# Taps of a 31-wide convolution on three engines, with sums in PSUM, and more first products in three passes

## The chip, the cores and the metric

The kernel runs on one core of a Trainium2 chip. The metric is device time in microseconds (us) for one execution, taken over several executions; the median is compared. A profiled execution of the same program gives the trace from which the rows below come. The engines are TensorE (PE, with its weight loads as PEld), VectorE (DVE), ScalarE (ACT), GpSimd (POOL) and SyncE (SP), which issues the loads.

## The reference

One inference step of a two-layer trunk on 256 prompt tokens and 8 sample tokens, 264 columns in all, of width 2048. Layer 0 mixes tokens with a Conformer convolution, layer 1 with a gated linear recurrence; each is followed by a convolutional feed-forward block of width 5632. The change touches the first mixer alone:

```python
def conformer_conv(x, buf, w_pw1, b_pw1, w_dw, b_dw, ln_g, ln_b, w_pw2, b_pw2):
    h = x @ w_pw1 + b_pw1                    # 2048 -> 4096
    a, gt = jnp.split(h, 2, axis=-1)
    u = a * jax.nn.sigmoid(gt)
    c, new_buf = causal_depthwise_conv(u, buf, w_dw, b_dw)   # 31 taps a channel
    c = jax.nn.silu(layernorm(c, ln_g, ln_b))
    return c @ w_pw2 + b_pw2, new_buf
```

The prompt starts with an empty history, so tap d of a prompt column reads the column d places earlier and nothing where that lies ahead of the prompt. Each sample token has its own history of 30 columns (buf), which enters as one weighted sum a channel.

## The kernel before, in words

Channels lie on the 128 partitions, so the 2048 channels are 16 tiles (KT) of 128 x 264 (T). Everything stays in SBUF between stages; weights stream in as 128 x 2048 blocks of 1 MB into three buffers (tag w), the loads issued by SyncE in one fixed order up to four slots ahead (LOADS).

A **slot** (L185) is one product of such a block with 16 slices. A weight in NATIVE is multiplied as fp32, 16 matmuls, each two records in the trace. Any other is split: ScalarE rounds it to a high part (split_hi, L139), VectorE subtracts to get the low part (split_lo, L151), and three passes of 16 matmuls run (high x high, high x low, low x high; L181 to L183), for which the right-hand side has to be in two parts too. In the stage of the change, all 32 first products (pw1) are native and all but two of the second products (pw2) are split.

For channel tile i there are two slots: the product a (index i) and the product for the gate (index 16 + i). After the matmuls of a slot the program issues what was registered with `later(n, ...)` (0 is the next slot, 1 the one after it): first the list "begin", then the casts of weights two slots ahead (AHEAD), then "early", then the low parts, then "late" (L198 to L206). The order on ScalarE, VectorE and TensorE is that order of issue, since the schedule is manual for them.

For tile i this is: sigmoid of the gate product (ScalarE, L366), the gate u = (a + b) x sigmoid (VectorE, L374), then the taps. One sum starts as ScalarE's scaling of u (L378), the other (part) on VectorE; 29 further taps (L409, L417) are VectorE's multiply-and-add, alternating between the two sums, in three groups over the next three slots; an addition joins the sums (L425, and its twin for the last tile, L421). The last tile, of which nothing can be put beside a product, has 17 of its taps (TE) on TensorE with diagonal weights, made by ScalarE beforehand (diagonals, L388; diagonal_taps, L395).

From tile 5 on, a mean m0 of the first four tiles is subtracted within the sums; the first five tiles have it subtracted in one block (catch_up, L449). Squares (ScalarE, L348) and two running sums (dsum and qsum, VectorE, L358 and L359) feed the LayerNorm, whose totals come from TensorE after the last tile (p_mu, L499). At the start, conv_state multiplies the sample history with the weights (L339) and reduces it over 30 places (L341), and normalise (L457 on) makes the 16 normalised right-hand sides xg, once the RMSNorm's scale is known; tile 0 is multiplied before that, by the unscaled xr.

PSUM has eight banks: six in one rotation (tag pt, L73), one for statistics (st), one (pl) for a transposed piece of the output at the very end. GpSimd does nothing in this stage.

Of the kernel before, what the change touches and what calls it, by code (L numbers as in the profile page):

```python
# [17 lines left out]
P = 128  # L18
# [5 lines left out]
CW = 31  # L24
# [20 lines left out]
NATIVE = {("pw1", n) for n in range(2 * KT)} | {("pw2", 0), ("pw2", 1), ("ho", 0)}  # L45
AHEAD = 2
LOADS = 4
TE = 17
# [14 lines left out]
def kernel(ctx: ExitStack, tc: tile.TileContext, a: dict):  # L63
    nc = tc.nc
    vec, act, pe = nc.vector, nc.scalar, nc.tensor
    ctx.enter_context(tc.manual_schedule(engines={mybir.EngineType.PE, mybir.EngineType.Activation, mybir.EngineType.DVE}))
# [20 lines left out]
    def pcol(name, i):  # L87
        c = COL[name] + i
        return par[:, c : c + 1]
# [134 lines left out]
    class Stats:  # L224
# [91 lines left out]
    with ExitStack() as ph:  # L316
        gp = ph.enter_context(tc.tile_pool(name="gp", bufs=1))
        cstate = gp.tile([P, KT, CW - 1, NB], F32, tag="cstate", name="cstate")
# [19 lines left out]
        def conv_state():  # L338
            vec.tensor_tensor(out=cstate, in0=cstate, in1=wall[:, :, : CW - 1].unsqueeze(3).to_broadcast((P, KT, CW - 1, NB)),  # L339
                              op=ALU.mult)  # L340
            vec.tensor_reduce(out=csum, in_=cstate.rearrange("p k j b -> p k b j"), axis=AX.X, op=ALU.add)  # L341

        NM = 4
        c, m = [], {}

# [22 lines left out]
        def glu(i, pa):  # L368
            sg = m.pop(("sg", i))
            u = gp.tile([P, T], F32, tag="u", name=f"u{i}", bufs=3)  # L370
# [3 lines left out]
            vec.scalar_tensor_tensor(out=u, in0=pa[:, :T], scalar=pcol("b_pw1", i), in1=sg, op0=ALU.add, op1=ALU.mult)  # L374
            m[i] = u
            ci = gp.tile([P, T], F32, tag=f"c{i}", name=f"c{i}")
            c.append(ci)
            act.activation(ci, u, AF.Identity, scale=pcol("w_dw", i * CW + CW - 1), bias=pcol("b_dw", i))  # L378
            act.copy(ulast[:, i, :], u[:, SEQ - CW + 1 :])
# [4 lines left out]
        def diagonals():  # L384
            free = [sp.tile([P, 2, P], F32, tag=f"l{k}", name=f"diag{k}") for k in range((TE + 1) // 2)]
            for j in range(TE):
                diag[j] = free[j // 2][:, j % 2, :]
                act.activation(diag[j], ident, AF.Identity, scale=pcol("w_dw", (KT - 1) * CW + j))  # L388

        def diagonal_taps():  # L390
            u = m[KT - 1]
            pt = m["pt"] = bank("p_taps")
            for j in range(TE - 1, -1, -1):
                d = CW - 1 - j
                pe.matmul(pt[:, d:SEQ], diag[j], u[:, : SEQ - d], start=(j == TE - 1), stop=(j == 0))  # L395

        def taps(i, lo, hi):

            u, ci = m[i], c[i]
            if hi == CW - 1:  # L400
                part = m["part", i] = gp.tile([P, T], F32, tag="part", name=f"part{i}", bufs=2)
                w = pcol("w_dw", i * CW + CW - 2)
                if i <= NM:
                    vec.memset(part[:, :1], 0.0)
                    vec.tensor_scalar(out=part[:, 1:SEQ], in0=u[:, : SEQ - 1], scalar1=w, scalar2=None, op0=ALU.mult)
                    vec.tensor_copy(part[:, SEQ:], csum[:, i, :])
                else:
                    m0 = m["m0"]
                    vec.scalar_tensor_tensor(out=part[:, 1:SEQ], in0=u[:, : SEQ - 1], scalar=w, in1=m0[:, 1:SEQ],  # L409
                                             op0=ALU.mult, op1=ALU.subtract)  # L410
                    vec.tensor_scalar(out=part[:, :1], in0=m0[:, :1], scalar1=-1.0, scalar2=None, op0=ALU.mult)
                    vec.tensor_tensor(out=part[:, SEQ:], in0=csum[:, i, :], in1=m0[:, SEQ:], op=ALU.subtract)
                hi -= 1
            for j in range(hi - 1, lo - 1, -1):
                d = CW - 1 - j
                dst = ci if d % 2 == 0 else m["part", i]
                vec.scalar_tensor_tensor(out=dst[:, d:SEQ], in0=u[:, : SEQ - d], scalar=pcol("w_dw", i * CW + j),  # L417
                                         in1=dst[:, d:SEQ], op0=ALU.mult, op1=ALU.add)
            if lo == TE and i == KT - 1:
                d = CW - TE  # L420
                vec.tensor_tensor(out=ci, in0=ci, in1=m.pop(("part", i)), op=ALU.add)  # L421
                vec.tensor_tensor(out=ci[:, d:SEQ], in0=ci[:, d:SEQ], in1=m["pt"][:, d:SEQ], op=ALU.add)
                square(i)
            elif lo == 0:
                vec.tensor_tensor(out=ci, in0=ci, in1=m.pop(("part", i)), op=ALU.add)  # L425
                if i > NM:
                    square(i)
# [35 lines left out]

        later(0, normalise, last=True)
        later(2, conv_state, last=True)
        for i in range(KT):
            first = i == 0
            if i == 1:
                nc.sync.dma_start(cst, a["cst"])
                nc.sync.dma_start(a["o_conv_old"], a["cs"][:, :, 1:, :])  # L470
            pa, = slot([("pw1", i)], None, xr if first else xg)
            pg, = slot([("pw1", KT + i)], None, xr if first else xg, ahead=AHEAD if i < KT - 1 else 0)
            later(0, lambda i=i, pg=pg: sigmoid(i, pg), first=True)
            later(0, lambda i=i, pa=pa: glu(i, pa))
            if i == KT - 1:
                later(0, diagonal_taps)
                later(0, lambda i=i: taps(i, TE, 30), last=True)
                continue
            later(0, lambda i=i: taps(i, 16, 30), last=True)
            later(1, lambda i=i: taps(i, 3, 16))  # L480
            later(2, lambda i=i: taps(i, 0, 3))
            later(2, lambda i=i: gathered(i), last=True)
# [8 lines left out]
        mu = gp.tile([P, T], F32, tag="mu", name="mu")  # L491
# [39 lines left out]
        hl = nxt  # L531

# [460 lines left out]
    with ExitStack() as ph:  # L993
# [11 lines left out]
        pl = ps.tile([P, 512], F32, tag="pl", name="p_y", bufs=1)  # L1005
# [10 lines left out]
        for i in range(2):  # L1016
            turn_back(i, 1, bank(f"p_y{i}_1") if i else pl)
# [113 lines left out]
```

## Time and profile before

| | us |
|---|---|
| median of 3 executions (2459.83 to 2460.58) | 2460.41 |
| the profiled execution's own time | 2459.5 |
| its span in the trace | 2457.7 |
| TensorE busy in the span | 2428.8 |
| VectorE busy | 1742.6 |
| ScalarE busy | 1127.8 |
| GpSimd busy | 0.2 |
| stage of the first products, from the first to the last of their matmuls on the chain | 17.36 to 238.63 |

The profiled execution has 1.8 us around its span. The 31-tap stage is less than a tenth of it: the feed-forward blocks take most of the time (2816 matmuls in each of three passes alone take 2399 us of busy records, which overlap). Records are matmuls, so a native product counts 32 and a split one 48. In rows of instructions the columns are the start of the first, the busy time of all in the row, the engine, the line of the kernel with the operation and its operands (output <- inputs, buffer numbers left out), and how many the row holds. Start-to-start spacings of a dense run tell more than durations do, since instructions of one engine overlap a little at their ends.

### The profile page before, as it was taken

How to read it: one execution, taken by the hardware profiler on the slowest of the kernel's cores; microseconds unless marked ns; L12 is line 12 of the kernel's file. 1: busy time of each engine (PE TensorE's matmuls, PEld its weight loads, DVE VectorE, ACT ScalarE, POOL GpSimd, SP SyncE). 2: the span in 40 equal slices, each digit the busy share in tenths (PEclk: the TensorE clock that was granted, in tenths of full speed). 3: DMA queues.
4: the chain of work that ended last, by engine and by line, in shares of the span. 5: the costliest groups of instructions: out<-in, count | busy, mean ns of one | idle time of the engine just before them, and what ended most of it. 6: DMA issues, size and time to landing. Idle time of an engine off the chain costs nothing.

```text
span 2457.7 us, 48532 instructions
## 1 busy us (share of the span) xinstructions
PE 2428.8 (99%) x20710; PEld 2376.4 (97%) x20710; DVE 1742.6 (71%) x3087; ACT 1127.8 (46%) x1841; POOL 0.2 (0%) x4
## 2 busy tenths in 40 slices
PE   8999899999999999999999999999999999999998
PEld 7888899999999999999999999999999999999998
DVE  8999867676566566567877777867767556657655
ACT  1112645544344345345766665544444344444434
POOL 0000000000000000000000000000000000000000
PEclk9999999999999999999999999999999999999999
DMA  7444455554554555556666565655555455465453
GB/s 271 153 144 152 157 187 191 187 173 161 194 193 164 180 190 177 173 177 207 227 209 213 202 214 194 210 177 200 179 182 179 155 206 183 154 208 177 165 179 129
DMA packets 78136, 453.04 MB, mean 184 GB/s; under 512 B 8544, under 2 KB 13024, under 8 KB 39008
## 3 DMA queue, kind: packets, MB, share of 16 engines
q1 hardware_dynamic: 77920, 449.94, 53.5%
q8 instruction: 162, 2.65, 0.4%
q14 instruction: 54, 0.44, 0.0%
HBM read 436.31 MB, written 15.50 MB: 184 GB/s over the span
## 4 chain that ended last, share of the span: by engine, by line
PE 87%; DVE 8%; ACT 3%; issue 1%; DMA 0%; DVEq 0%; SPq 0%; ACTq 0%
PE p_up L183 14%; PE p_up L181 14%; PE p_up L182 14%; PE p_pw L178 10%; PE p_dn L183 7%; PE p_dn L182 7%; PE p_dn L181 7%; DVE R L703 2%; PE p_ho L181 1%; PE p_ho L182 1%; PE p_ho L183 1%; PE p_pw L182 1%; PE p_pw L181 1%; PE p_pw L183 1%; DVE wl_hq L151 1%; DVE wl_hi L151 1%
## 5 line engine op out<-in xcount | busy, mean ns | idle before, releaser
L181 PE MATMUL p_up<-h_ffn,wh_up 128*128 128x264 f32 x2816 | 801.0, 284 | 0.0
L183 PE MATMUL p_up<-h_ffn,wl_up 128*128 128x264 f32 x2816 | 800.7, 284 | 0.0
L182 PE MATMUL p_up<-l_ffn,wh_up 128*128 128x264 f32 x2816 | 797.5, 283 | 0.0
L139 ACT CAST wh_up<-w_up 128x2048 fp32r<-128x2048 f32 x176 | 336.3, 1911 | 505.3 <-PE p_up L182 446.3
L151 DVE TENSOR_TENSOR wl_up<-w_up,wh_up 128x2048 fp32r<-128x2048 f32 x176 | 403.6, 2293 | 232.2 <-ACT wh_up L139 232.2
L181 PEld LDWEIGHTS p_up<-h_ffn,wh_up 128*128 128x128 f32 x2816 | 530.1, 188 | 0.1
L183 PEld LDWEIGHTS p_up<-h_ffn,wl_up 128*128 128x128 f32 x2816 | 530.0, 188 | 0.0
L182 PEld LDWEIGHTS p_up<-l_ffn,wh_up 128*128 128x128 f32 x2816 | 529.6, 188 | 0.1
L183 PE MATMUL p_dn<-gh,wl_dn 128*128 128x264 f32 x1408 | 400.8, 285 | 0.0
L181 PE MATMUL p_dn<-gh,wh_dn 128*128 128x264 f32 x1408 | 400.3, 284 | 0.0
L182 PE MATMUL p_dn<-gl,wh_dn 128*128 128x264 f32 x1408 | 400.1, 284 | 0.0
L139 ACT CAST wh_dn<-w_dn 128x1408 fp32r<-128x1408 f32 x128 | 176.1, 1375 | 325.7 <-PE p_dn L182 243.6
L151 DVE TENSOR_TENSOR wl_dn<-w_dn,wh_dn 128x1408 fp32r<-128x1408 f32 x128 | 208.1, 1626 | 108.4 <-ACT wh_dn L139 108.4
L182 PEld LDWEIGHTS p_dn<-gl,wh_dn 128*128 128x128 f32 x1408 | 265.3, 188 | 0.0
L183 PEld LDWEIGHTS p_dn<-gh,wl_dn 128*128 128x128 f32 x1408 | 264.7, 188 | 0.0
L181 PEld LDWEIGHTS p_dn<-gh,wh_dn 128*128 128x128 f32 x1408 | 264.6, 188 | 0.0
L178 PE MATMUL p_pw<-xg,w_pw 128*128 128x264 f32 x960 | 213.9, 386 | 0.0
L178 PEld LDWEIGHTS p_pw<-xg,w_pw 128*128 128x128 f32 x960 | 182.4, 190 | 31.2
L569 DVE SCALAR_TENSOR_TENSOR C<-H,par,C 128x255 f32<-128x255 f32 x352 | 169.3, 481 | 6.3
L280 DVE TENSOR_TENSOR x<-x,p_dn 128x264 f32<-128x264 f32 x128 | 54.9, 429 | 111.7 <-PE p_dn L183 111.7
L563 DVE TENSOR_TENSOR H<-p_up,rstd_ffn 128x264 f32<-128x264 f32 x176 | 76.1, 432 | 77.7 <-PE p_up L183 77.7
L564 ACT ACTIVATE C<-H,par 128x264 f32<-128x264 f32 x176 | 105.9, 601 | 13.9 <-DVE H L563 13.9
(320 smaller groups left out, 3988.5 us busy)
## 6 DMA issues: line engine op xcount, KB each, us to landing
w_up<-in_up SPq DMA_DIRECT2D x176, 1024.0 KB
w_dn<-in_dn SPq DMA_DIRECT2D x128, 704.0 KB
w_pw<-in_pw SPq DMA_DIRECT2D x47, 1024.0 KB
w_hf<-in_hf SPq DMA_DIRECT2D x16, 1024.0 KB
w_hq<-in_hq SPq DMA_DIRECT2D x16, 1024.0 KB
w_hi<-in_hi SPq DMA_DIRECT2D x16, 1024.0 KB
w_hg<-in_hg SPq DMA_DIRECT2D x16, 1024.0 KB
w_ho<-in_ho SPq DMA_DIRECT2D x16, 1024.0 KB
```

Of the source, the lines that this page charges most:

```text
L139: act.copy(wh[:, :kk, :], raw[key][:, :kk, :])
L151: vec.tensor_tensor(out=wl[:, :kk, :], in0=raw.pop(key)[:, :kk, :], in1=wh.bitcast(F32)[:, :kk, :], op=ALU.subtract)
L178: pe.matmul(pt[:, :T], wh[:, k, :], full[k], start=(k == 0), stop=last)
L181: pe.matmul(pt[:, :T], wh[:, k, :], rh, start=(k == 0), stop=False)
L182: pe.matmul(pt[:, :T], wh[:, k, :], rl, start=False, stop=False)
L183: pe.matmul(pt[:, :T], wl[:, k, :], rh, start=False, stop=last)
L280: vec.tensor_tensor(out=x[n], in0=x[n], in1=pt[:, :T], op=ALU.add)
L563: vec.tensor_tensor(out=h, in0=pt[:, :T], in1=rstd, op=ALU.mult)
L564: act.activation(cc, h, AF.Identity, scale=wv[:, j, 2:3], bias=pcol("ffn_b", layer * 2 * FT + j))
L569: vec.scalar_tensor_tensor(out=cc[:, d:SEQ], in0=h[:, : SEQ - d], scalar=wv[:, j, 2 - d : 3 - d], in1=cc[:, d:SEQ], op0=ALU.mult, op1=ALU.add)
L703: vec.tensor_tensor(out=new, in0=old, op=ALU.mult, in1=g.rearrange("p r n s -> p r (n s)").unsqueeze(3).to_broadcast((P, 2, 2 * n, b)))
```

## The change

18 of the 32 first products leave NATIVE: the gate products of tiles 3 to 15 and the a products of tiles 5, 7, 9, 11 and 13 (SPLIT). Their weights are cast by ScalarE and subtracted by VectorE, and xg gets a high part (16 casts on ScalarE, high_parts) and a low part (16 subtractions on VectorE, low_parts), issued two and three slots after the first.

The 31 taps of a tile are divided. ScalarE begins two sums in two PSUM banks, even (tap 0 with the bias) and odd (tap 8, columns from 8 on). VectorE adds taps 1 to 7 to the one and 9 to 15 to the other, alternating, in the PSUM banks. Taps 16 to 30 are ScalarE's: it makes 15 products of 240 columns each in SBUF, in pairs (two, more), and GpSimd adds the pairs up into far. VectorE then closes the tile: it copies even to SBUF (or subtracts m0 from it), adds odd, the sample history and far (end_sums). So that a tap can read ahead of the prompt, the three buffers of u carry 30 columns of zeros. The last tile has taps 1 to 12 on VectorE, 13 to 18 on ScalarE and GpSimd, 19 to 30 on TensorE with twelve diagonals.

The banks are divided accordingly during this stage: three for products (pt), two each for even and odd, one for statistics. After the stage the pool of six is taken again, and the bank of the last piece of the output is allocated only where it is used. The reduction over 30 places in conv_state becomes a tree of seven additions. mu takes the buffer of far. GpSimd's order is manual too.

```diff
+SPLIT = {KT + i for i in range(3, KT)} | {i for i in range(5, KT - 1, 2)}
+NATIVE = {("pw1", n) for n in range(2 * KT) if n not in SPLIT} | {("pw2", 0), ("pw2", 1), ("ho", 0)}
...
+ODD = 8
+FAR = 16
+FAR_LAST, FAR_PE = 13, 19
...
-    ps = ctx.enter_context(tc.tile_pool(name="ps", bufs=6, space=PSUM))
+        ps = ph.enter_context(tc.tile_pool(name="ps_conv", bufs=3, space=PSUM))
...
-            vec.tensor_reduce(out=csum, in_=cstate.rearrange("p k j b -> p k b j"), axis=AX.X, op=ALU.add)
+            n = CW - 1
+            while n > 1:
+                half = n // 2
+                vec.tensor_tensor(out=cstate[:, :, :half, :], in0=cstate[:, :, :half, :],
+                                  in1=cstate[:, :, half : 2 * half, :], op=ALU.add)
+                if n % 2:
+                    vec.tensor_tensor(out=cstate[:, :, 0, :] if half > 1 else csum, in0=cstate[:, :, 0, :], in1=cstate[:, :, n - 1, :], op=ALU.add)
+                n = half
...
+        us = [gp.tile([P, CW - 1 + T], F32, tag=f"u{i}", name=f"u{i}") for i in range(3)]
+        for t in us:
+            pool.memset(t[:, : CW - 1], 0.0)
...
+        def tap(i, dst, d, first):
+            vec.scalar_tensor_tensor(out=dst[:, d - first : SEQ - first], in0=m[i][:, : SEQ - d], scalar=weight(i, d),
+                                     in1=dst[:, d - first : SEQ - first], op0=ALU.mult, op1=ALU.add)
+        def begin_sums(i):
+            u = m[i]
+            even = m["even", i] = ps.tile([P, 512], F32, tag="even", name=f"even{i}", bufs=2)[:, :T]
+            odd = m["odd", i] = ps.tile([P, 512], F32, tag="odd", name=f"odd{i}", bufs=2)[:, : SEQ - ODD]
+            act.activation(even, u, AF.Identity, scale=weight(i, 0), bias=pcol("b_dw", i))
+            act.activation(odd, u[:, : SEQ - ODD], AF.Identity, scale=weight(i, ODD))
...
+        def products(i, n):
+            top, two, padded = SEQ - m["two", i].shape[-1], m["two", i], us[i % 3]
+            for lo, hi in m["products", i][:n]:
+                out = two
+                if lo > top:
+                    out = gp.tile([P, 2, SEQ - FAR_LAST], F32, tag="more", name=f"more{i}_{lo}", bufs=2)[:, :, : SEQ - top]
+                for d in range(lo, hi):
+                    act.activation(out[:, d - lo, :], padded[:, CW - 1 + top - d : CW - 1 + SEQ - d], AF.Identity, scale=weight(i, d))
+                if lo > top:
+                    pool.tensor_tensor(out=two[:, : hi - lo, :], in0=two[:, : hi - lo, :], in1=out[:, : hi - lo, :], op=ALU.add)
+            m["products", i] = m["products", i][n:]
+            if not m["products", i]:
+                far = m["far", i] = gp.tile([P, T], F32, tag="far", name=f"far{i}", bufs=2)[:, top:SEQ]
+                pool.tensor_tensor(out=far, in0=two[:, 0, :], in1=two[:, 1, :], op=ALU.add)
...
+        def end_sums(i):
...
+            if i > NM:
+                yield vec.tensor_tensor(out=ci, in0=even, in1=m["m0"], op=ALU.subtract)
+            else:
+                yield vec.tensor_copy(ci, even)
+            yield vec.tensor_tensor(out=ci[:, ODD:SEQ], in0=odd, in1=ci[:, ODD:SEQ], op=ALU.add)
+            yield vec.tensor_tensor(out=ci[:, SEQ:], in0=ci[:, SEQ:], in1=csum[:, i, :], op=ALU.add)
+            yield vec.tensor_tensor(out=ci[:, top:SEQ], in0=ci[:, top:SEQ], in1=far, op=ALU.add)
+            if i == KT - 1:
+                yield vec.tensor_tensor(out=ci[:, FAR_PE:SEQ], in0=ci[:, FAR_PE:SEQ], in1=m["pt"][:, FAR_PE:SEQ], op=ALU.add)
...
+        def low_parts():
+            xhl[:] = [low(k, xg[k], xhl[k], "xg") for k in range(KT)]
...
         later(2, conv_state, last=True)
+        later(2, high_parts, last=True)
+        later(3, low_parts)
...
-            later(0, lambda i=i, pa=pa: glu(i, pa))
+            later(0, lambda i=i, pa=pa: (glu(i, pa), begin_sums(i)))
...
+            later(0, lambda i=i: products(i, 4))
+            later(0, near_taps, last=True)
+            later(1, lambda i=i: (products(i, CW), list(taps(i, CW))))
+            if i == KT - 2:
+                later(1, lambda i=i: (finish_sums(i), square(i), gathered(i)), last=True)
+                continue
+            if i > NM:
+                later(3, lambda i=i: square(i), first=True)
+            later(3, lambda i=i: gathered(i))
...
             if i == NM:
-                later(2, catch_up, last=True)
+                later(3, catch_up, last=True)
```

near_taps issues eight taps of tile i, with the closing instructions of tile i - 1 between them.

Three places show how the order moves. On VectorE, near the start of the stage: the rows that stand just ahead of the gate of tile 1 (u1 <- p_pw1_1, whose reading frees a product's bank). l_xg are low parts of the right-hand side, even0 and odd0 the sums of tile 0 in PSUM, par holds the tap weights; the end of a row is the shape. In the changed kernel:

```order
L273 TENSOR_TENSOR l_xg_14_421<-xg14_257,h_xg_14_362 128x264
L273 TENSOR_TENSOR l_xg_15_423<-xg15_259,h_xg_15_364 128x264
L398 SCALAR_TENSOR_TENSOR even0_307<-u0_188,par_67,even0_307 128x251
L398 SCALAR_TENSOR_TENSOR odd0_308<-u0_188,par_67,odd0_308 128x243
L398 SCALAR_TENSOR_TENSOR even0_307<-u0_188,par_67,even0_307 128x250
L398 SCALAR_TENSOR_TENSOR odd0_308<-u0_188,par_67,odd0_308 128x242
L398 SCALAR_TENSOR_TENSOR even0_307<-u0_188,par_67,even0_307 128x249
L398 SCALAR_TENSOR_TENSOR odd0_308<-u0_188,par_67,odd0_308 128x241
L389 SCALAR_TENSOR_TENSOR u1_189<-p_pw1_1_282,par_67,sg1_467 128x264
L447 COPY c0_490<-even0_307 128x264
```

Of the kernel before, the same place on VectorE, where the taps run on down to 226 columns:

```order
L417 SCALAR_TENSOR_TENSOR part0_306<-u0_298,par_70,part0_306 128x227
L417 SCALAR_TENSOR_TENSOR c0_301<-u0_298,par_70,c0_301 128x226
L425 TENSOR_TENSOR c0_301<-c0_301,part0_306 128x264
L374 SCALAR_TENSOR_TENSOR u1_380<-p_pw1_1_276,par_70,sg1_374 128x264
L404 MEMSET part1_385 128x1
L405 TENSOR_SCALAR part1_385<-u1_380,par_70 128x255
```

The gate of tile 1 stands behind all taps of tile 0 in both; 15 fewer of them are VectorE's now, and the 16 low parts have come in between them.

On VectorE again, at the gate of tile 7 (which writes the second of the three buffers of u), in the changed kernel; wl_pw1_24 and wl_pw1_9 are the low parts of two weights, m0 is the mean of the first four tiles:

```order
L155 TENSOR_TENSOR wl_pw1_24_1323<-w_pw1_24_1157,wh_pw1_24_1296 128x2048
L389 SCALAR_TENSOR_TENSOR u1_189<-p_pw1_7_1156,par_67,sg7_1344 128x264
L155 TENSOR_TENSOR wl_pw1_9_1369<-w_pw1_9_1244,wh_pw1_9_1346 128x2048
L445 TENSOR_TENSOR c6_1371<-even6_1211,m0_1036 128x264
L398 SCALAR_TENSOR_TENSOR even7_1350<-u1_189,par_67,even7_1350 128x255
L448 TENSOR_TENSOR c6_1371<-odd6_1212,c6_1371 128x248
L398 SCALAR_TENSOR_TENSOR odd7_1351<-u1_189,par_67,odd7_1351 128x247
L449 TENSOR_TENSOR c6_1371<-c6_1371,csum_186 128x8
L398 SCALAR_TENSOR_TENSOR even7_1350<-u1_189,par_67,even7_1350 128x254
L450 TENSOR_TENSOR c6_1371<-c6_1371,far6_1315 128x240
```

Subtractions of 2048 columns now stand on both sides of the gate, and the closing of tile 6 lies between the first taps of tile 7; its last row waits for GpSimd's far6.

On ScalarE, at the end of the stage, ahead of the sigmoid of the last tile (sg15), in the changed kernel; more14 are pairs of far products of tile 14, sq_ln_14 its square for the LayerNorm:

```order
L425 ACTIVATE more14_24_2515<-u2_190,par_67 128x240 x2
L425 ACTIVATE more14_26_2519<-u2_190,par_67 128x240 x2
L425 ACTIVATE more14_28_2523<-u2_190,par_67 128x240 x2
L425 ACTIVATE more14_30_2527<-u2_190,par_67 128x240
L363 ACTIVATE sq_ln_14_2543<-c14_2538 128x264
L381 ACTIVATE sg15_2547<-p_pw1_31_2460,par_67 128x264
L391 COPY ulast_187<-u0_188 128x38
L406 ACTIVATE even15_2551<-u0_188,par_67 128x264
L407 ACTIVATE odd15_2552<-u0_188,par_67 128x248
```

and before:

```order
L348 ACTIVATE sq_ln_13_1500<-c13_1395 128x264
L378 ACTIVATE c14_1504<-u14_1502,par_70 128x264
L379 COPY ulast_187<-u14_1502 128x38
L366 ACTIVATE sg15_1558<-p_pw1_31_1526,par_70 128x264
L348 ACTIVATE sq_ln_14_1564<-c14_1504 128x264
L378 ACTIVATE c15_1568<-u15_1566,par_70 128x264
```

The sigmoid of tile 15 stood ahead of the square of tile 14 and now stands behind it, and behind the far products of tile 14; that square reads c14, which VectorE closes with GpSimd's far14.

More of the change, by code (lines that the diff above doesn't have):

```diff
@@ L375, in glu, with weight @@
             m[i] = u
+            act.copy(ulast[:, i, :], u[:, SEQ - CW + 1 :])
+        def weight(i, d):
+            return pcol("w_dw", i * CW + CW - 1 - d)
+        def tap(i, dst, d, first):
[7 more added lines that the diff above has]
+            act.activation(odd, u[:, : SEQ - ODD], AF.Identity, scale=weight(i, ODD))
+            last = i == KT - 1
+            top, end = (FAR_LAST, FAR_PE) if last else (FAR, CW)
+            m["two", i] = gp.tile([P, 2, SEQ - FAR_LAST], F32, tag="two", name=f"two{i}")[:, :, : SEQ - top]
+            m["products", i] = [(d, min(d + 2, end)) for d in range(top, end, 2)]
+            near = [d for d in range(1, ODD)], [d for d in range(ODD + 1, top)]
+            while len(near[1]) > len(near[0]) + 1:
+                near[0].append(near[1].pop())
+            m["taps", i] = [t for pair in zip_longest(*near) for t in ((even, pair[0], 0), (odd, pair[1], ODD)) if t[1]]
@@ L376, in glu, with taps @@
+        def taps(i, n):
+            while m["taps", i] and n:
+                yield tap(i, *m["taps", i].pop(0))
+                n -= 1
+        def end_sums(i):
+            assert not m.pop(("taps", i)) and not m.pop(("products", i))
+            even, odd, far = m.pop(("even", i)), m.pop(("odd", i)), m.pop(("far", i))
+            top = SEQ - far.shape[-1]
             ci = gp.tile([P, T], F32, tag=f"c{i}", name=f"c{i}")
             c.append(ci)
-            act.activation(ci, u, AF.Identity, scale=pcol("w_dw", i * CW + CW - 1), bias=pcol("b_dw", i))
@@ L382, with finish_sums @@
+            if i == KT - 1:
+                yield vec.tensor_tensor(out=ci[:, FAR_PE:SEQ], in0=ci[:, FAR_PE:SEQ], in1=m["pt"][:, FAR_PE:SEQ], op=ALU.add)
+        def finish_sums(i, between=iter(())):
+            for _ in end_sums(i):
+                next(between, None)
         diag = {}
         def diagonals():
[L385 to L388, printed above, removed]
+            free = gp.tile([P, CW - FAR_PE, P], F32, tag="cstate", name="diag")
+            for d in range(FAR_PE, CW):
+                diag[d] = free[:, d - FAR_PE, :]
+                act.activation(diag[d], ident, AF.Identity, scale=weight(KT - 1, d))
@@ L392, in diagonal_taps @@
             pt = m["pt"] = bank("p_taps")
[L393 to L427, printed above, removed]
+            for d in range(FAR_PE, CW):
+                pe.matmul(pt[:, d:SEQ], diag[d], u[:, : SEQ - d], start=(d == FAR_PE), stop=(d == CW - 1))
         def gathered(i):
@@ L490 @@
         upto("load", load, cnt["use"] + 3)
-        mu = gp.tile([P, T], F32, tag="mu", name="mu")
+        mu = gp.tile([P, T], F32, tag="far", name="mu", bufs=2)
         var = sp.tile([P, T], F32, tag="nv", name="var")
@@ L531 @@
         hl = nxt
+    ps = ctx.enter_context(tc.tile_pool(name="ps", bufs=6, space=PSUM))
     def conv_ffn(layer, hl, rs, scale):
@@ L1016 @@
         for i in range(2):
-            turn_back(i, 1, bank(f"p_y{i}_1") if i else pl)
+            turn_back(i, 1, ps.tile([P, 512], F32, tag="pl", name=f"p_y{i}_1", bufs=1))
         steps, r = [], []
```

29 lines of the change are left out of this document (15 added, 14 removed).

## The prediction

> **What bounds the kernel now.** I read the page first, then the chain of work that ended last in the first tenth of the span, then windows over that stage, then the order of time on VectorE and ScalarE.
>
> ```profile
> span 2457.7 us, 48532 instructions
> ...
> PE 2428.8 (99%) x20710; PEld 2376.4 (97%) x20710; DVE 1742.6 (71%) x3087; ACT 1127.8 (46%) x1841; POOL 0.2 (0%) x4
> ...
> DVE  8999867676566566567877777867767556657655
> ...
> 17.36 78.32 PE p_pw L178 x352
> ...
> 96.13 142.41 PE p_pw L178 x640
> 238.63 0.49 ACT sg L366
> 239.14 0.50 DVE u L374
> 239.69 7.00 PE p_taps L395 x34
> 246.71 0.42 DVE c L422
> 247.17 0.71 PE p_mu L499 x2
> ```
>
> TensorE is the whole chain: from 17.4 to 238.6 us the first products (p_pw) follow each other with nothing between them but one 0.45 us sum. Only then, from 238.6 to 247.2, does the chain leave TensorE: sigmoid, gate, the taps of the last channel tile, its closing sum. VectorE is over 90% busy in the very slices of this stage (one digit is 61 us), so shorter products help only if VectorE's work shrinks too.
>
> ```profile
> core 0: us, PE busy (x) PEld busy (x) DVE busy (x) ACT busy (x) POOL busy (x), PEclk, DMA share, GB/s
> 24.00:238.00 214.00, 214.00 (x964) 182.74 (x963) 212.79 (x562) 28.69 (x77) 0.00 (x0) 1.00 0.47 161
> 283.00:343.00 60.00, 60.00 (x497) 60.00 (x496) 38.43 (x44) 27.85 (x33) 0.00 (x0) 1.00 0.58 196
> ```
>
> A native product of 16 slices is 32 records. In the chain 640 records took 142.4 us: 7.12 us a product. The second window holds products in three passes, 48 records each: 497 in 60 us, 5.79 us a product. The granted clock is 1.00 in both. ScalarE is idle for 185 of 214 us, GpSimd for all of them.
>
> **The products.** 18 of 32 become three-pass: 18 x (7.12 - 5.79) = **-24.0 us**, if nothing holds TensorE. The rest of this part is what holds it.
>
> **What the engines do for each channel tile.** Spacings, start to start, and durations:
>
> ```profile
> 160.47 0.42 DVE L358 TENSOR_TENSOR dsum<-dsum,c 128x264 f32<-128x264 f32 x1
> 160.81 0.43 DVE L359 TENSOR_TENSOR qsum<-qsum,sq_ln 128x264 f32<-128x264 f32 x1
> ...
> 161.69 0.47 DVE L417 SCALAR_TENSOR_TENSOR c<-u,par,c 128x254 f32<-128x254 f32 x1
> 162.09 0.47 DVE L417 SCALAR_TENSOR_TENSOR part<-u,par,part 128x253 f32<-128x253 f32 x1
> ...
> 282.76 2.29 DVE L151 TENSOR_TENSOR wl_pw<-w_pw,wh_pw 128x2048 fp32r<-128x2048 f32 x1
> ...
> 160.59 0.61 ACT L378 ACTIVATE c<-u,par 128x264 f32<-128x264 f32 x1
> 161.10 0.21 ACT L379 COPY ulast<-u 128x38 f32<-128x38 f32 x1
> 213.58 5.08 ACT L388 ACTIVATE diag<-cst,par 128x128 f32<-128x128 f32 x17
> ...
> 280.32 1.90 ACT L139 CAST wh_pw<-w_pw 128x2048 fp32r<-128x2048 f32 x1
> ...
> L388 ACT ACTIVATE diag<-cst,par 128x128 f32<-128x128 f32 x17 | 5.1, 390 | 0.0
> ...
> L262 ACT ACTIVATE h_ffn<-x,par 128x264 fp32r<-128x264 f32 x6 | 3.0, 503 | 0.0
> ```
>
> A tap costs VectorE 0.39, an addition 0.34. Before, a tile of 30 taps held it some 13 us. Now it is 14 taps (5.45), the gate (0.40), four closing instructions (1.1), two statistics (0.69) and 2.2 for the subtraction of each split weight: 9.9 us with one such weight, 12.1 with two, 22.0 for two tiles. On ScalarE 17 scalings of 128 columns take 5.08, spaced 0.29; from 128 to 264 columns a scaling grows from 390 to 503 ns, so one of 240 columns is spaced 0.39, and the fifteen far products of a tile take 5.8. With sigmoid, two beginnings in PSUM (0.5 and 0.4), copy, square and three casts of 1.9, two tiles are 21.0. TensorE needs 24.5 for two tiles (7.12 + 3 x 5.79). Both engines fit, by 2.5 and 3.5 us.
>
> Writing PSUM from VectorE or ScalarE is in no row. The gate reads PSUM and lasts what an SBUF tap lasts per column (0.49 for 264, 0.47 for 254; row below), so I take no difference. Five hundredths either way on 14 taps are 0.7 us a tile: +4 at the stage's end when it goes against the slack, -1 the other way.
>
> GpSimd adds six times 480 and twice 240 columns for each tile. The trace has no GpSimd arithmetic, only constants:
>
> ```profile
> L1122 POOL MEMSET const-float32-0.0<- 128x1 f32 x1 | 0.1, 99 | 0.2 <-issue 0.2
> ...
> 33.85 7.05 DVE L341 TENSOR_REDUCE csum<-cstate 128x128 f32<-128x3840 f32 x1
> ```
>
> The nearest rows are VectorE's: its addition at 480 columns would be 0.57 us (2.29 for 2048); its slowest line per column, the reduction, has 1.84 ns, which is 0.88 us. I take 1.0, a little over the upper row, because each sum also waits for the one ahead of it and for ScalarE; 0.57 and 1.4, as far on the other side, go into the rivals. That is 7.1 us for a tile of 12.2: it fits.
>
> The Trainium skill (GPSIMD Engine Reference, Performance versus the Vector engine) gives 2293 ns for an addition of 2048 columns on VectorE, which this trace has too (2.29), and 4497 ns on GpSimd, which no row here shows; scaled, its estimate is 1.05 to 1.15 us, by which the sum would come out 2 to 4 us later than mine.
>
> **What is late next.** I laid the lists of the four engines side by side, each instruction at the later of its engine's turn and its input. TensorE is held in three places, all through the banks for products, 6 before and 3 now: a product waits until the gate or the sigmoid has read the bank of the product three before it.
>
> ```profile
> 29.26 0.49 DVE L374 SCALAR_TENSOR_TENSOR u<-u,par,sg 128x264 f32<-128x264 f32 x1 [0.24 <-ACT sg L366]
> 29.67 4.15 DVE L339 TENSOR_TENSOR cstate<-cstate,par 128x3840 f32<-128x3840 f32 x1
> ...
> 52.64 0.49 DVE L374 SCALAR_TENSOR_TENSOR u<-p_pw,par,sg 128x264 f32<-128x264 f32 x1
> ...
> 24.32 7.95 PE L178 MATMUL p_pw<-xg,w_pw 128*128 128x264 f32 x35
> ...
> 269.17 5.58 DVE L269 TENSOR_TENSOR lows<-c,h_ln 128x264 fp32r<-128x264 f32 x16
> ...
> 103.60 0.77 DVE L449 TENSOR_TENSOR c<-c,m 128x264 f32<-128x264 f32 x2
> ...
> 108.79 0.47 DVE L409 SCALAR_TENSOR_TENSOR part<-u,par,m 128x255 f32<-128x255 f32 x1
> ```
>
> *Opening.* The gate of tile 1 came at 52.6 and hurt nobody: six banks. Now the sixth product, due at 24.2 + 3 x 7.12 = 45.5, needs the bank that this gate reads. VectorE ahead of the gate: the multiply until 33.85, seven additions in place of the reduction (3712 columns 3.9, seven hand-overs 1.3), 8 taps 3.1, 16 low parts 5.6, 6 taps 2.3, so 50.0, and the gate until 50.5. **+5.1.** (The additions save 1.9 against the reduction; the low parts cost 5.6.)
>
> *Catch-up.* The block from 103.60 to 108.79 is 5.2 us of VectorE at one go. Its tile now holds 12.1 + 5.2 - 0.7 = 16.6 us for 12.9 of products; the banks cover about 1.3 of the difference: **+2.4**. Waits of 0.2 in other tiles: together **+0.7**.
>
> *End.* ScalarE makes twelve diagonals (3.5 us) among the products of tile 13, so the gate of tile 14 comes just as the last product starts. From that gate on, ScalarE needs 2.6 us until the first two pairs are there, GpSimd 7.1 for its sums, VectorE 0.9 to close c14 and start the statistics, ScalarE 0.9 for its square and the sigmoid of tile 15, which stands behind that square, and VectorE 0.5: the last gate ends 12.0 after the one before, 6.2 after the last product. In the chain above that is 1.0 (238.63 to 239.64). **+5.2.** From there the two are alike: 12 taps on TensorE for 17 (4.9 for 7.0), on VectorE 1.3 until the beginnings stand, 11 taps 4.4 and dependent additions 1.9: 7.5, against 7.5 from 239.64 to 247.17. **0.**
>
> Behind 247.2 only banks change: a residual addition (0.49) has 5.8 us there, and the hand-over to the later pool costs the feed-forward one such evacuation at most. Loads are the same in number and order; their bytes over 190 us are 181 GB/s, less than the 196 of the second window, and between a load's start and the first use of a split weight lie two products, over 11 us.
>
> **Sum:** -24.0 + 5.1 + 2.4 + 0.7 + 5.2 = -10.6. On the profiled execution's 2459.5 us (the span and 1.8 around it) that is 2448.9; the median of the runs lies 0.9 above that execution: **2450 us**.
>
> **Rivals.**
>
> *GpSimd and VectorE exclude each other.* GpSimd and VectorE never run side by side in this trace, so no row speaks for or against a shared port. Suppose an instruction of VectorE with two inputs in SBUF and an addition of GpSimd cannot run together. The taps have one input in PSUM and go free; the split subtractions, two closing additions and the two statistics do not, 11 instructions in two tiles. GpSimd runs 58% of the time, and one that meets it waits half an addition: 11 x 0.29 = 3.2 us, against 2.5 of slack; and their 8.8 us stop GpSimd in turn, on which ScalarE's two buffers and so the sigmoids wait. Laid side by side again, two tiles take 28 instead of 24.5: four times 3.5, 3 more in the opening (multiply, additions and low parts all have two inputs), 7.5 around the catch-up, 0.5 at the end: +25, **2475 us**. It is slower than before once this costs over 11 us, under half of what is counted here.
>
> The Trainium skill (SBUF — State Buffer, Who interferes with whom) states this rule, the second to start being blocked until the first ends; no run here shows it, and by it the time would be that of this rival.
>
> *GpSimd is the bound.* At 1.4 us an addition ScalarE's two buffers hold its products back and each gate comes later: 1.9 for each of three pairs of tiles, 2.6 at the catch-up, 6 at the end: +14, 2464. The two kernels meet at about 1.35 us. For it speaks that the sums are a chain; against it the rows, which end at 0.88.
>
> *GpSimd is quick.* At 0.57 the end costs 0.3 and the catch-up 1.6: -24.0 + 5.1 + 1.6 + 0.3 = -17, **2443 us**. More is not there: no GpSimd sum stands in the opening.
>
> **How the numbers follow.** Forecast 0.53 (2445 to 2456), quick 0.12, GpSimd the bound 0.11, exclusion 0.24, since nothing here bears on it and it takes so little to tip the sum. Runs of this kernel differ by 0.03%; two kernels can be told apart from about 0.2%, 5 us. Forecast and quick are faster: 0.65. Half of GpSimd-the-bound and a little of the exclusion are the same: 0.08; slower 0.27. The range goes from the quick case with the gain in PSUM and some room, 2438, to the exclusion's price, 2476.
>
> **What would show it.** Right: split products at 120 ns a record; one hole of 5 us before the sixth product, released by the gate of tile 1; VectorE's taps 0.39 apart; GpSimd's additions 1 us apart; a hole of 6 us before the diagonal taps. Wrong: two-input VectorE instructions that wait or run on beside GpSimd, GpSimd additions over 1.3 us, or a hole before every second product, released by a gate. Taps in PSUM at 0.45 would put the time near 2455.

## The result, and the profile after

| | before | after |
|---|---|---|
| median of all executions, us | 2460.12 (2458.74 to 2460.58) | 2489.98 (2489.62 to 2490.74) |
| ratio, 95% interval | | 1.0123 (1.0105 to 1.0140) |
| span of the profiled execution | 2457.7 | 2487.8 |
| last first product ends | 238.6 | 260.1 |
| last tile closed (p_mu on c starts) | 247.2 | 276.0 |

The change makes the kernel 1.2% slower; 2450 was forecast, with a range from 2438 to 2476. Of the 30.1 us between the spans, 21.5 arise among the first products, 7.3 between the last of them and the closing of the last tile (15.9 us, where it was 8.6), and 1.3 behind that. From the page of the changed kernel:

```profile
span 2487.8 us, 49467 instructions
...
PE 2423.6 (97%) x20988; PEld 2383.7 (96%) x20988; DVE 1725.5 (69%) x2901; ACT 1261.5 (51%) x2117; POOL 164.1 (7%) x130
```

TensorE has 5 us less to do than the 2428.8 before, VectorE 17 less, although time in which an instruction is held up counts as busy: the work did shrink. What TensorE waits for in the stage, by the view of waits (total, times, longest):

```profile
PE p_pw L185 <- ACT sg L381: 26.2, 10, 8.8
PE p_taps L471 <- DVE u L389: 7.5, 1, 7.5
...
PE p_pw L187 <- DVE wl_pw L155: 2.2, 3, 0.8
PE p_pw L182 <- DVE u L389: 1.7, 1, 1.7
```

Thirty microseconds of holes stand among products that had none, nearly all released by a sigmoid: 6.7 in the opening, 8.8 at the catch-up, 14.6 in the other tiles. Beside the holes, records run slower: the six three-pass products behind the holes of 2.1 us and more take 7.5 to 8.3 us each where the forecast has 5.79, 11.5 us together. With small gaps (3.9) that makes 15.4, and the 21.5 are -24.0 + 30.1 + 15.4. Why the sigmoids are late is read from the chain of waits between two gates, on the longest pieces (start, us, what):

```profile
189.05 0.42 DVE u L389
189.71 0.48 ACT even L406
190.20 0.71 POOL two L427
190.99 0.71 POOL far L431
191.72 0.88 ACT two L425 x2
192.60 0.79 ACT more L425 x2
193.52 1.23 POOL two L427
194.78 0.88 ACT more L425 x2
195.97 1.79 ACT wh_pw L143
197.76 0.79 ACT more L425 x2
198.69 3.31 POOL two L427
202.07 1.21 POOL two L427
203.31 0.49 ACT more L425
```

Right behind the last row stands the sigmoid, here in ScalarE's timeline:

```profile
203.31 0.49 ACT L425 ACTIVATE more<-u,par 128x240 f32<-128x240 f32 x1 [0.40 <-POOL two L427]
203.71 0.46 ACT L381 ACTIVATE sg<-p_pw,par 128x264 f32<-128x264 f32 x1
```

TensorE isn't in this chain, and not in the rest of it between 28.7 and 267.6 us either; so by the chain the slow records lie inside time that other engines set. ScalarE's products wait for GpSimd to empty a buffer, GpSimd waits for products, a cast stands between, and the sigmoid, which TensorE needs, is queued behind the products. The gates of tiles 10 and 12 start at 188.97 and 219.28: two tiles take 30.3 us where their products need 24.5.

One row is strange: an addition of 3.31 us beside others of 1.21. GpSimd's timeline at that place (start, us, instruction), and under it VectorE's, there and at the closing of tile 8:

```profile
198.69 3.30 POOL L427 TENSOR_TENSOR two<-two,more 128x480 f32<-128x480 f32 x1 [1.18 <-ACT more L425]
```

```profile
179.94 1.23 DVE L450 TENSOR_TENSOR c<-c,far 128x240 f32<-128x240 f32 x1
181.10 0.47 DVE L398 SCALAR_TENSOR_TENSOR odd<-u,par,odd 128x246 f32<-128x246 f32 x1
...
198.65 2.28 DVE L155 TENSOR_TENSOR wl_pw<-w_pw,wh_pw 128x2048 fp32r<-128x2048 f32 x1
```

The subtraction began 0.04 us ahead of the addition, ran its usual 2.28, and the addition took 2.1 longer than alone. At 179.94 it is the other way round: VectorE's addition of far takes 1.23 while GpSimd adds (0.40 at 192.03, where GpSimd is idle). The taps run on at 0.39 apart. Grouped over the stage (count, busy us, mean ns), for VectorE:

```profile
L155 DVE TENSOR_TENSOR wl_pw<-w_pw,wh_pw 128x2048 fp32r<-128x2048 f32 x18 | 44.3, 2459 | 6.6 <-ACT wh_pw L143 6.6
L450 DVE TENSOR_TENSOR c<-c,far 128x240 f32<-128x240 f32 x15 | 10.2, 678 | 2.8 <-POOL far L431 2.8
L373 DVE TENSOR_TENSOR dsum<-dsum,c 128x264 f32<-128x264 f32 x14 | 7.7, 552 | 0.0
L398 DVE SCALAR_TENSOR_TENSOR even<-u,par,even 128x254 f32<-128x254 f32 x16 | 7.6, 478 | 0.0
...
L448 DVE TENSOR_TENSOR c<-odd,c 128x248 f32<-128x248 f32 x16 | 6.6, 411 | 0.1
```

Instructions with both inputs in SBUF are longer than their like before (the dsum addition took 0.42 to 0.43 before, 0.55 on the mean now), those with one input in PSUM are not (a tap 0.47 before and now, the addition of odd 0.41). One copy from SBUF to SBUF was long too (dsum at 124.88, 0.78 us against 0.30 without GpSimd's sums). In such a meeting one engine waits for the other's instruction to end. The Trainium skill (SBUF — State Buffer, Who interferes with whom) states this: an instruction of VectorE with two inputs in SBUF contends with one of GpSimd that reads SBUF, and the ports that they share are an exclusive lock; the trace agrees, with 3.30 and 1.23 us.

### The profile page after: what moved, and what is told of

Read it like the earlier page. It is cut to its first block, busy times and chain, and to the rows that moved or that the text cites. A ratio compares the mean times of both kernels' runs of the same rounds, so it can differ in the third digit from the quotient of the medians.

```text
span 2487.8 us, 49467 instructions
## 1 busy us (share of the span) xinstructions
PE 2423.6 (97%) x20988; PEld 2383.7 (96%) x20988; DVE 1725.5 (69%) x2901; ACT 1261.5 (51%) x2117; POOL 164.1 (7%) x130
## 4 chain that ended last, share of the span: by engine, by line
PE 77%; DVE 12%; ACT 6%; POOL 3%; issue 2%; DMA 1%; SPq 0%; POOLq 0%; DVEq 0%; ACTq 0%
PE p_up L187 14%; PE p_up L185 14%; PE p_up L186 14%; PE p_dn L187 7%; PE p_dn L186 7%; PE p_dn L185 7%; POOL two L427 2%; DVE R L771 2%; PE p_ho L185 1%; PE p_ho L187 1%; PE p_ho L186 1%; PE p_pw L185 1%; PE p_pw L186 1%; PE p_pw L187 1%; PE p_pw L182 1%
## 5 line engine op out<-in xcount | busy, mean ns | idle before, releaser
L427 POOL TENSOR_TENSOR two<-two,more 128x480 f32<-128x480 f32 (+2 forms) x107 | 152.4, 1424 | 107.8 <-ACT more L425 101.8
L185 PE MATMUL p_pw<-h_xg,wh_pw 128*128 128x264 f32 x288 | 88.4, 307 | 26.2 <-ACT sg L381 26.2
```

What stands on the lines that cost most here:

```text
L185: pe.matmul(pt[:, :T], wh[:, k, :], rh, start=(k == 0), stop=False)
L427: pool.tensor_tensor(out=two[:, : hi - lo, :], in0=two[:, : hi - lo, :], in1=out[:, : hi - lo, :], op=ALU.add)
```

## The experiments

Times are medians; "span" is the profiled execution's. The kernel before ran beside them, with medians of 2459.55 to 2459.73; spans are compared with its 2457.7 and the change's 2487.8.

**Without GpSimd's additions.** Of the far products only the first of the first pair enters the sum, the rest are made and not added. The edit:

```diff
-                if lo > top:
-                    pool.tensor_tensor(out=two[:, : hi - lo, :], in0=two[:, : hi - lo, :], in1=out[:, : hi - lo, :], op=ALU.add)
...
-                pool.tensor_tensor(out=far, in0=two[:, 0, :], in1=two[:, 1, :], op=ALU.add)
+                m["far", i] = two[:, 0, :]
```

> The changed kernel without any of GpSimd's additions: far is the first product of the pair alone, so the other 14 far products of a tile are made by ScalarE and dropped. Theory (GpSimd's additions, at 1.21 us each and shutting VectorE's two-input instructions out and being shut out by them, are the loss): the end of the last closing sum falls from 275.9 to about 229 us, because products and VectorE then run at their own pace, and the span from 2487.8 to about 2441. Rival (sums in PSUM, three banks for products, or ScalarE's work hold TensorE): the span stays above 2465, with the same holes in front of products.

Measured: span 2458.0, median 2459.19, ratio to before 0.9998 (0.9989 to 1.0007). The loss goes, but 17 us of the expected gain don't come. The edit had put in a wait of its own: in ScalarE's timeline the first pair of the next tile now waits for VectorE to have read the last one, 3.6 us at a time.

```profile
188.88 0.89 ACT L425 ACTIVATE two<-u,par 128x240 f32<-128x240 f32 x2 [3.59 <-DVE c L447]
```

So it was run again with a second buffer for that pair (in the space of the sample history):

```diff
+            m["two", i] = (second_two() if i > 1 and i % 2 else gp.tile([P, 2, SEQ - FAR_LAST], F32, tag="two", name=f"two{i}"))[:, :, : SEQ - top]
```

> As the run without GpSimd's additions, but with two buffers for the first pair of far products, so that ScalarE's next pair doesn't wait until VectorE has read the last one, a wait which that run had put in. Theory (without GpSimd's sums nothing else of the change holds TensorE but the end): the last closing sum near 224 to 228, the span 2435 to 2440. Rival (ScalarE's order or the three banks hold it too): two tiles still take over 26 us, the span is above 2450.

Measured: span 2439.3, median 2441.44, ratio 0.9928 (0.9914 to 0.9941). TensorE's waits shrink to

```profile
PE p_pw L185 <- ACT sg L381: 2.2, 2, 1.1
PE p_taps L477 <- DVE u L389: 1.1, 1, 1.1
```

and two tiles take 24.66 (native products start at 143.11, 167.77, 192.43), against the 24.5 of the sum. Three banks, sums in PSUM and ScalarE's products hold next to nothing (2.2 us of holes); GpSimd's additions, with what they block and what waits for them, are worth 48.5 us, in a kernel with the second buffer.

**Subtractions out of the exclusion.** The second operand of the 18 subtractions comes from PSUM, 128 columns of zeros, repeated, so that what it writes is no longer the low part:

```diff
+            other = zero[0][:, 384:512].unsqueeze(1).to_broadcast((P, kk, P)) if key[0] == "pw1" else wh.bitcast(F32)[:, :kk, :]
-            vec.tensor_tensor(out=wl[:, :kk, :], in0=raw.pop(key)[:, :kk, :], in1=wh.bitcast(F32)[:, :kk, :], op=ALU.subtract)
+            vec.tensor_tensor(out=wl[:, :kk, :], in0=raw.pop(key)[:, :kk, :], in1=other, op=ALU.subtract)
```

> The changed kernel with the subtraction for the low part of each first weight reading its second operand from PSUM (a 128-column piece repeated 16 times) in place of the high part in SBUF: the low part is wrong, length and order of the instruction are the same. Theory (VectorE's instructions with two inputs in SBUF and GpSimd's additions exclude each other, the 18 subtractions of 2.2 us most of all): additions of 3.3 us disappear from GpSimd's rows, the last closing sum ends near 253 instead of 275.9, the span is near 2465. Rival (GpSimd's 1.21 us and ScalarE's two buffers make a serial chain, exclusion or not): additions next to a subtraction may be shorter, the span stays within 4 us of 2487.8.

Measured: span 2464.7, median 2465.34, ratio 1.0025 (1.0015 to 1.0034). GpSimd's group in the changed kernel, then in this one:

```profile
L427 POOL TENSOR_TENSOR two<-two,more 128x480 f32<-128x480 f32 (+2 forms) x107 | 152.4, 1424 | 107.8 <-ACT more L425 101.8
```

```profile
L430 POOL TENSOR_TENSOR two<-two,more 128x480 f32<-128x480 f32 (+2 forms) x107 | 131.7, 1231 | 104.5 <-ACT more L428 98.5
```

and the subtractions themselves, 2459 on the mean in the changed kernel:

```profile
L156 DVE TENSOR_TENSOR wl_pw<-w_pw,st_conv 128x2048 fp32r<-128x2048 f32 x18 | 41.0, 2280 | 0.0
```

The same 107 additions, of which not one was touched, lose 20.7 us, and the time falls by 23.1. In the changed kernel 19 additions of 480 columns run beside a subtraction, and 13 of them take 2.46 to 3.31 us; here 28 do, and 27 of them take 1.20 to 1.24. That one operand's place decides this shows the exclusion. Two tiles now take 25.8 us (the gates of tiles 8, 10 and 12 start at 148.72, 174.53 and 200.30). The 23.1 isn't the price of the exclusion alone: the subtraction no longer reads the high part, so that VectorE's waits for ScalarE's casts go too (6.6 us in the row of the changed kernel, at most 1.3 at a time, 0.0 here).

**No three-pass products.** `SPLIT = set()`; the rest of the change stays.

> The changed kernel with all 32 first products native, as before the change: no casts and no subtractions of first weights, everything else of the change stays. Theory (each part holds TensorE by itself): GpSimd's chain still needs more than a native pair at the end and in the catch-up, the opening wait stays; the last closing sum ends near 256, 8 us later than before the change, the span is near 2467. Rival (only the subtractions on VectorE hurt): the taps alone fit under 14.2 us of native products, the span is within 4 us of the 2457.7 of before.

Measured: span 2465.2, median 2465.92, ratio 1.0026 (1.0016 to 1.0036). The taps' division costs 7.5 us even under native products, but not where the theory put it. TensorE waits 1.7 and 2.7 us before the seventh and the eighth product, both in the opening. From there on the chain shows its products without a hole:

```profile
64.67 44.67 PE p_pw L182 x192
109.78 135.29 PE p_pw L182 x608
```

The first 192 records take 2.0 us longer than at 7.12 us for 32, the other 608 don't. So the last product ends 6.5 us later. The way from it to the closing is as long as before (8.4 us against 8.6), the catch-up costs nothing, and 1.2 us arise behind the stage.

**More buffers between ScalarE and GpSimd.**

```diff
-                    out = gp.tile([P, 2, SEQ - FAR_LAST], F32, tag="more", name=f"more{i}_{lo}", bufs=2)[:, :, : SEQ - top]
+                    out = gp.tile([P, 2, SEQ - FAR_LAST], F32, tag="more", name=f"more{i}_{lo}", bufs=2) if i < 2 or (lo // 2) % 5 < 2 else spare(i, lo)
```

> The changed kernel with five buffers for the later pairs of far products in place of two, and two for the first pair in place of one (the additional ones lie where the sample history was). Theory (exclusion makes GpSimd late, and lateness reaches TensorE because ScalarE, and the sigmoid queued behind its products, waits for a buffer): ScalarE's waits for GpSimd shrink, the last closing sum ends near 257 instead of 275.9, the span is near 2469. Rival (GpSimd's own sums set each gate through the closing sums, buffers or not): the span stays within 5 us of 2487.8.

Measured: span 2466.2, median 2467.94, ratio 1.0033 (1.0021 to 1.0045). With nothing made shorter (the edit also gives the first pair a second buffer), 21.6 us come back: GpSimd's lateness reaches TensorE through ScalarE's queue. No run moved the sigmoid ahead of the products instead.

**Shorter additions.** One product of each later pair is added instead of two:

```diff
-                    pool.tensor_tensor(out=two[:, : hi - lo, :], in0=two[:, : hi - lo, :], in1=out[:, : hi - lo, :], op=ALU.add)
+                    pool.tensor_tensor(out=two[:, :1, :], in0=two[:, :1, :], in1=out[:, :1, :], op=ALU.add)
```

> The changed kernel with the second product of each later pair left out of GpSimd's sums: additions of 240 columns instead of 480, as many of them; ScalarE makes all products. Theory (GpSimd's time is on the loop through ScalarE's buffers, so that each microsecond of it counts): additions of 0.7 us, six of them save some 3 us a tile on GpSimd, the last closing sum near 252, the span near 2464. Rival (it is the number of meetings with VectorE's instructions that counts, not GpSimd's time): the span within 6 us of 2487.8.

Measured: span 2453.7, median 2455.90, ratio 0.9985 (0.9976 to 0.9994); 10 us better than expected, though an addition takes 1043 ns on the mean (0.70 where nothing blocks it), since the meetings remain. The length of GpSimd's additions counts as well as the exclusion. The three gains (23.1, 21.6, 34.1) are ways into one loop and don't add up.

**The clock at the end.** Fourteen spare matmuls in the last hole:

```diff
+            warm = bank("p_warm")
+            for k in range(14):
+                pe.matmul(warm[:, :T], ones, xg[k], start=(k == 0), stop=(k == 13))
```

> The changed kernel with 14 additional matmuls (ones by xg into a bank that nobody reads) on TensorE in the hole of 7.5 us ahead of the diagonal taps. Theory (the twelve diagonal taps take 7.9 us, 0.33 us a record instead of the 0.206 of before, because TensorE's granted clock is at half after the hole): with TensorE busy until the gate they take about 5 us, and the closing sum comes up to 3 us sooner, as far as VectorE's own taps (until about 274) let it: the span falls by 1 to 2. Rival (the diagonals or the shapes make them slow): 7.9 us as before, no change of the span.

Measured: span 2486.9, median 2488.98, ratio 1.0121 (1.0105 to 1.0136). The diagonal taps in the changed kernel, and here:

```profile
L471 PE MATMUL p_taps<-u,diag 128*128 128x237 f32 (+11 forms) x24 | 7.9, 511 | 7.5 <-DVE u L389 7.5
```

```profile
L474 PE MATMUL p_taps<-u,diag 128*128 128x237 f32 (+11 forms) x24 | 5.0, 362 | 0.7 <-DVE u L389 0.7
```

7.9 becomes 5.0, so the hole had cost 3 us of clock. The span falls by only 0.9, no more than executions of the changed kernel differ by (spans of 2487.8 to 2489.0): VectorE's own taps and additions end 1.2 us ahead of the slow diagonal taps, so no more could be won.

**The banks at the very end.** As before the change, the second pair of output pieces gets two banks:

```diff
-            turn_back(i, 1, ps.tile([P, 512], F32, tag="pl", name=f"p_y{i}_1", bufs=1))
+            turn_back(i, 1, bank(f"p_y{i}_1") if i else ps.tile([P, 512], F32, tag="pl", name="p_y", bufs=1))
```

> The changed kernel with two banks for the second pair of output pieces at the very end, as before the change (the change puts both through the single bank pl). Theory (TensorE's wait of 3.3 us for ScalarE there, 1.0 before the change, delays the last copies): that wait is back at 1.0 and the span falls by about 1 us from 2487.8. Rival (the last stores hide it): no change.

Measured: span 2486.2, median 2488.85, ratio 1.0120 (1.0104 to 1.0135). The wait, in the changed kernel and here:

```profile
PE p_y L1071 <- ACT y L1098: 3.3, 1, 3.3
```

```profile
PE p_y L1071 <- ACT y L1098: 1.0, 1, 1.0
```

The wait is back at 1.0. Of the 1.6 us between the two spans, 1.1 arise ahead of the closing of the last tile (274.9 against 276.0), where the edit changes nothing; 0.5 at most are its own, less than two executions differ by. So only the wait is shown.

**An eased version, and one with its end mended.** The first:

```diff
-SPLIT = {KT + i for i in range(3, KT)} | {i for i in range(5, KT - 1, 2)}
+SPLIT = {KT + i for i in range(4, KT - 1)}
-FAR = 16
+FAR = 20
...
-            if i == KT - 3:
-                later(0, diagonals, last=True)
+            if 5 <= i <= 10:
+                later(1, lambda i=i: diagonals(FAR_PE + 2 * (i - 5)), last=True)
```

> A version drawn from the runs: only the gate products of tiles 4 to 14 in three passes (11 instead of 18), 11 far products a tile instead of 15 (taps 1 to 19 on VectorE), two buffers for the first pair, the diagonals made two a tile in tiles 5 to 10 instead of all in tile 13, the low parts a slot later. Theory (both engines then have slack for the exclusion): 11 x 1.33 = 14.6 us of products less some 6 of remaining holes, the last closing sum near 238, 9 before that of the kernel before: the span near 2449 against 2457.7. Rival (any work of GpSimd beside VectorE in this stage costs more than three passes save): not below 2457.

Measured: span 2456.0, median 2459.05, ratio 0.9997 (0.9988 to 1.0006): no change that can be told, where 2449 was expected. Two holes of 1.5 are left among the products, and the last product ends 7.9 us earlier than before the change. But the end holds 4.7, after which the diagonal taps take 7.25: 3.8 us are lost again up to the closing, and 2.4 behind it. The second, on top of it (with three spare matmuls and two banks for the last pieces, as in the runs above):

```diff
-FAR_LAST, FAR_PE = 13, 19
+FAR_LAST, FAR_PE = 11, 17
-        later(4, low_parts)
+        later(4, low_parts, last=True)
-                later(0, lambda i=i: (products(i, CW), list(taps(i, CW)), finish_sums(i), square(i)), last=True)
+                later(0, lambda i=i: (finish_sums(i - 1), products(i, CW), square(i - 1), list(taps(i, CW)), finish_sums(i), square(i)), last=True)
...
+            pe.matmul(pt[:, :T], ones, late, start=False, stop=False)
```

> The eased version with its end mended: the gate of tile 15 stands ahead of the closing of tile 14; tile 14's sum and square go straight into the LayerNorm's totals on TensorE; fourteen diagonals and ten VectorE taps for the last tile instead of twelve and twelve, three spare matmuls ahead of the diagonal taps; the low parts stand behind the gate of tile 1; the last two pieces of the output have two banks again. Theory (what is left over is the end, the opening wait and the end banks): 1.5 from the opening, about 3 from the end, about 1 from the banks: the span near 2451, 0.25% faster than the kernel before. Rival (VectorE, not the order, sets the end): less than 2 us below the eased version's 2456.0.

Measured: span 2452.2, median 2454.14, ratio 0.9978 (0.9969 to 0.9987), 0.22% faster than the kernel before, and the best of the versions that leave nothing out. Its edits were not tried one by one. TensorE's timeline at its end, and the stage by a window (the busy time of PE, PEld, VectorE, ScalarE and GpSimd, with instructions):

```profile
230.91 1.50 PE L479 MATMUL p_warm<-xg,ones 128*128 128x264 f32 x6
233.48 5.76 PE L482 MATMUL p_taps<-u,big 128*128 128x239 f32 x28 [1.07 <-DVE u L389]
```

```profile
24.00:231.00 207.00, 202.80 (x1142) 180.94 (x1141) 200.81 (x422) 122.20 (x281) 105.45 (x89) 1.00 0.46 167
```

VectorE is busy for 200.8 of 207 us, which leaves little room for the subtractions of more products in three passes; none was tried.

## Why the prediction was wrong, point by point

The forecast went by work for each tile: VectorE 22.0 and ScalarE 21.0 us for two tiles of 24.5, GpSimd 7.1 for a tile of 12.2, each called a fit. From this it put all waits in tiles other than the opening and the catch-up at +0.7. That term is the step that failed: it measured 14.6 us of holes, and two tiles took 30.3 us. The waits that it left out are ScalarE's for GpSimd and, behind them in ScalarE's queue, the sigmoid's; the exclusion, which the prediction had as a rival, makes GpSimd late. With what the other terms measured:

| | forecast | measured |
|---|---|---|
| products | -24.0 | -24.0 by the same sum |
| holes in the opening | +5.1 | +6.7 |
| hole at the catch-up | +2.4 | +8.8 |
| holes in the other tiles | +0.7 | +14.6 |
| slow records and small gaps | not in the sum | +15.4 |
| from the last product to the closing | +5.2 | +7.3 |
| behind the stage | 0 | +1.3 |
| all | -10.6 | +30.1 |

The rows are an account of TensorE's time and not of causes: where the loop sets the pace, slow records only fill what would be a hole.

- **The products**: right. Where nothing holds them (the run without sums, two buffers), two tiles took 24.66 us for the 24.5 of the sum.
- **VectorE's and ScalarE's shares**: taps in PSUM at 0.39, as taken. What failed is "both engines fit, by 2.5 and 3.5 us": shares of busy time were compared, while sigmoid, products, buffers and sums are one loop through three engines.
- **GpSimd's 1.0 us**: mis-sized, 1.21 measured (0.71 for 240 columns). The estimate from the Trainium skill (GPSIMD Engine Reference, Performance versus the Vector engine), 1.05 to 1.15, was nearer. By the rival "GpSimd is the bound", which met the kernel before at about 1.35, 1.21 alone would still have been faster.
- **The rival "GpSimd and VectorE exclude each other"** had the mechanism, and the forecast was chosen over it with 0.53 to 0.24. The exclusion is shown. Its price, 2475, was worked out with additions of 1.0 us; the long additions and the exclusion were priced apart and never together. Together they come to some 2482 by the prediction's own figures (an estimate: 14 us for 1.4 in place of 1.0, so 7 for 1.21), past the range's 2476 and still short of 2490.
- **The opening, +5.1**: wrong in its reason. The timeline of TensorE (its last row is cut off by the view's end at 60 us):

```profile
7.34 9.59 PE L182 MATMUL p_pw<-xr,w_pw 128*128 128x264 f32 x32 [7.34 <-DVE acc_mix L248]
17.21 7.28 PE L182 MATMUL p_pw<-xr,w_pw 128*128 128x264 f32 x32
24.33 28.64 PE L182 MATMUL p_pw<-xg,w_pw 128*128 128x264 f32 x128
54.70 5.61 PE L182 MATMUL p_pw<-xg,w_pw 128*128 128x264 f32 x24 [1.73 <-DVE u L389]
```

  Six products run through before the gate of tile 1 (54.15, late by 4 because GpSimd blocks the tree and the low parts, 7.24 for 5.6); the seventh waits 1.7, and the eighth, whose bank a sigmoid behind ScalarE's products frees, 5.0 more. The prediction's "no GpSimd sum stands in the opening" was wrong: those of tile 0 run there from 32.54 on. Without them the gate of tile 1 starts at 49.98, as forecast. Banks are handed out in the order in which the program frees them, and the sigmoid of a tile frees one ahead of its gate.
- **The catch-up, +2.4**: its hole is 8.8, the longest; VectorE's instructions with two inputs in SBUF stand there in a row (the five subtractions of m0 took 422 to 1424 ns, 722 on the mean, 426 before), and the sigmoid that ends the hole stands behind the five squares that wait for them. Without GpSimd's sums, with the second buffer, 1.1 is left of it.
- **The end, +5.2**: 7.3 up to the closing. The hole ahead of the diagonal taps was forecast at 6 and is 7.5; that the taps would be slow after it was left out, 3 us on TensorE, of which at most 1.2 reached the closing.
- **Behind the stage, 0**: 1.3. That both pieces of the output now share one bank was overlooked: 2.3 us more of waiting; the hand-over of the pool costs 0.7. Together they are more than the 1.3, so part of the waiting is hidden; with two banks 0.8 is left.

How the loss divides between the additions' length and the exclusion stays open: no run had additions of 1.21 us that nothing blocked. The run with subtractions from PSUM comes nearest, with two tiles in 25.8 us where the changed kernel takes 30.3 and the products 24.5, but it has the casts' waits gone too. What a full clock alone would gain within the stage wasn't tried either; by the chain it would be little, which isn't shown.

## What to carry to other kernels

Work that is moved to an idle engine has to be priced as a loop, with the buffers on the way, the queue it stands in and whom it blocks, not as a share of busy time. In this kernel VectorE beside a busy GpSimd kept its pace where one operand was in PSUM; where both are in SBUF, count the other engine's instruction into each meeting. Two uncertain prices that lie in one loop are priced together, at the bad end of both. What TensorE needs next (here the sigmoid) should go ahead of anything that can wait for a third engine; this is drawn from the chain, no run tried it within the stage.

## What the hardware showed beside that

TensorE's granted clock drops after short holes, in this case's traces. In the windows of the changed kernel (PE busy and records, PEld, VectorE, ScalarE, GpSimd, then the granted clock):

```profile
67.00:72.00 5.00, 4.93 (x22) 4.93 (x23) 4.52 (x13) 3.53 (x10) 3.01 (x4) 0.50 0.37 154
72.00:77.00 5.00, 5.00 (x36) 4.77 (x35) 5.00 (x9) 4.24 (x7) 4.15 (x3) 0.98 0.00 0
```

After the hole of 5.0 us that ends at 67.07, records run at half pace for 5 us. It happened after six holes of the products and the one at the end, down to 2.1 us long, not after those of 1.7 and less, and not after one of 2.3 in the mended version (granted clock 1.00 there). The Trainium skill (TensorE: Matmul & The Clock Gate, What's actually happening) names a free-running window of 3.4 us for both directions. That a hole of 2.1 has the effect and one of 2.3 has not fits a window that runs freely; that 2.1 is enough doesn't fit an idle window of 3.4.
